# Two attention stages of a diffusion block: projections handed out in eighths behind the transposes, and scores that span two PSUM banks

## The chip, the cores and the metric

The kernel runs on one core of one Trainium2 chip. The metric is the time of one execution on the device, in microseconds (us). Three runs of the kernel before gave 2849.23, 2852.33 and 2855.4 us; their median, 2852.33 us, is the time to beat.

A core has five engines that work side by side, each through a queue of its own: TensorE (PE in the profile, with its weight loads as PEld), VectorE (DVE), ScalarE (ACT), GpSimd (POOL), and SyncE (SP), which issues transfers. TensorE writes to PSUM, which has eight banks of 512 float32 columns for each of 128 partitions. Semaphores order the engines among each other.

## The reference

Two layers run over 512 latent tokens and 256 context tokens of width 1024. Each layer has a feed-forward part, an attention part and another feed-forward part; the first layer's attention is grouped attention in a window, the second's is differential attention. Cut to what the change touches:

```python
def _gqa_window_mixer(...):            # 16 query heads, 4 key heads, 64 wide
    kx, vx = proj_kv(hx); kc, vc = proj_kv(hc)
    kx = _apply_rope(kx, cos, sin)
    qx = _apply_rope(proj_q(hx), cos, sin)
    # per block of 128 queries: 384 keys around it, and all of the context
    p = sink_softmax(concatenate([s_loc, s_ctx]))
    return einsum(p[..., :span], vb) + einsum(p[..., span:], vc)   # then @ w_out

def _diff_attn_mixer(...):             # 8 heads of two 64-wide halves, all 768 keys
    p = softmax(s * 64 ** -0.5)
    p = p[:, :, 0] - lam * p[:, :, 1]
    o = _rmsnorm(p @ v, subln_w) * (1.0 - lambda_init)             # then @ w_out
```

Everything is float32. The kernel gets this precision from TensorE by splitting an operand into a rounded high part and a low remainder, so that a product of two split operands takes three matmuls.

## The kernel before, in words

All activations lie transposed, 128 features on the partitions by 768 tokens (256 of the context, then 512), eight such blocks. xh and xl are the two parts of the normalized input. A projection (project_halves, line 265) makes 128 output features: weights() (line 48) loads 128 by 1024 weights on SP's queue (line 54), ScalarE rounds them (line 55) and GpSimd takes the remainder (line 56); then, for each half of the tokens, 8 blocks k times 3 products are summed in one PSUM bank. VectorE scales the bank by the norm (scaled_halves, line 288), and rope() (line 306) turns queries and keys.

**Grouped attention** (gqa, line 321) has eight PSUM banks in four pools: one bank for projections and outputs (pbig, tiles "half"), two for transposes, one for values, four for scores. The loop (line 556) runs 24 steps: 4 key groups by 6 blocks of 128 queries (4 latent, 2 context). In step i the scores of step i + 1 are traced first (scores, line 411), then a whole projection or a unit of the output projection if the tables of lines 539 to 541 name one for this step, then the values of step i (values, line 458). scores() makes up to two chunks for each of four heads, with maximum (line 434), exponential (line 441) and a normalization, three heads of four on GpSimd (line 454). values() takes the blocks of keys that the table XB (line 402) lists: four transposes (line 466), a rounded copy on ScalarE (line 469), the remainder on VectorE (line 470), two matmuls (lines 471 and 472). At step 18 xh and xl are given up, hT is loaded in their place (line 561), and the finished outputs of the first two groups come back from DRAM (line 501). out_proj (line 508) multiplies them by the output weights and adds into hT (line 302).

**Differential attention** (diff, line 586) has the same eight banks. For each of 8 heads the four query blocks' probabilities (probs, line 668) alternate with the next head's projections of keys, queries and values. A block has two score sets (j = 0, 1) of 768 keys, in two chunks of 384, a bank each. The maxima (line 680) are joined and scaled (line 683), each chunk is exponentiated (line 686), the sums are joined and inverted (lines 690 to 692), GpSimd scales the second set (line 694) and VectorE adds the two (line 695). values() (line 698) transposes and multiplies, and ends in a norm of the output, four operations of it on GpSimd (lines 721 to 724). For the last head parts of the output projection stand in place of projections. rope() has its sine product on GpSimd here (line 315).

**The order of the work.** The order on every engine's queue is fixed ahead of the run by a planner: it runs an estimate of the program and lets each engine take the first-traced instruction that is ready by that estimate, so work traced late can be issued early where its inputs and buffers allow. A tile is given out again when its readers are done. With issue_after(x) the instructions traced in a block are placed behind x on x's engine, without waiting for x to end.

## Time and profile before

| what | value |
|---|---|
| median of three runs | 2852.33 us (2849.23 to 2855.4) |
| the profiled execution's own time | 2853.44 us |
| span of the profile, first to last instruction | 2851.6 us |
| granted TensorE clock, mean | 0.991 |
| TensorE busy | 2759.4 us, 97% of the span |
| VectorE busy | 1525.4 us, 53% |
| GpSimd busy | 1279.3 us, 45% |
| ScalarE busy | 962.6 us, 34% |
| last stage of grouped attention's loop ends near | 920 us |
| differential attention stands at about | 2060 to 2470 us |

A row of the profile names the line of the kernel, the engine, the operation, and the tiles it writes and reads; times are microseconds unless a mean is given, which is in nanoseconds. A matmul's busy time overlaps the next one's, so a busy TensorE is not always one at its peak. A wait is put down to the semaphore that came last. The granted clock of TensorE is given as a share of full speed.

### The profile page before, as it was taken

Reading aid. Unit: us, or ns where it says so; the run is one execution under the profiler, and the core shown is the slowest. Engines: PE = TensorE matmul, PEld = TensorE weight load, DVE = VectorE, ACT = ScalarE, POOL = GpSimd, SP = SyncE. Lnnn points to the kernel's source line nnn. Section 1 sums busy time; section 2 is a strip of 40 time slices with the busy share of each in tenths; the row PEclk is TensorE's granted clock in tenths of the full one; section 3 lists DMA queues with packets and bytes.
Section 4 is the critical chain, followed back from the end, with each engine's and each line's share of the span. In section 5 each row is a group of like instructions: output and inputs, shape, how many; then the busy total and the mean of one; then the engine's idle time right before and its main releaser. Section 6 shows DMA issues by size and latency. Waiting matters only on the chain. (4 is left out here: it accounts for less than half of the span.)

```text
span 2851.6 us, 40866 instructions
## 1 busy us (share of the span) xinstructions
PE 2759.4 (97%) x16162; PEld 2578.0 (90%) x16162; DVE 1525.4 (53%) x2661; ACT 962.6 (34%) x1733; POOL 1279.3 (45%) x756
## 2 busy tenths in 40 slices
PE   6999999999899999999999999999999999899998
PEld 4999999989777999999999999999988887799998
DVE  8645455567887844444557333333567777422223
ACT  3212112245666422121233221221345655422223
POOL 1434333365433533333444434333555665555553
PEclk9999999999999999999999999999999999999999
DMA  7332432342331223223323233233232233233331
GB/s 277 107 127 97 140 111 98 123 138 81 84 127 38 89 85 117 86 85 121 94 81 111 84 104 102 71 115 115 73 99 82 82 90 121 73 100 93 101 103 45
DMA packets 105119, 290.09 MB, mean 102 GB/s; under 512 B 12512, under 2 KB 22880, under 8 KB 104928
## 3 DMA queue, kind: packets, MB, share of 16 engines
q1 hardware_dynamic: 104496, 287.37, 31.3%
q8 instruction: 128, 2.10, 0.3%
q14 instruction: 63, 0.52, 0.1%
q10 hardware_dynamic: 432, 0.11, 0.0%
HBM read 257.28 MB, written 12.06 MB: 94 GB/s over the span
## 5 line engine op out<-in xcount | busy, mean ns | idle before, releaser
L56 POOL TENSOR_TENSOR w_lo<-w_raw,w_hi 128x1024 fp32r<-128x1024 f32 (+2 forms) x377 | 804.1, 2133 | 1089.8 <-ACT w_hi L55 1066.9
L55 ACT CAST w_hi<-w_raw 128x1024 fp32r<-128x1024 f32 (+2 forms) x377 | 337.5, 895 | 1112.4 <-PE big L70 398.2
L257 PE MATMUL big<-xh,w_hi 128*128 128x384 f32 (+3 forms) x2816 | 689.8, 326 | 6.5 <-DVE xh L174 3.2
L257 PE MATMUL big<-xh,w_lo 128*128 128x384 f32 (+3 forms) x2816 | 688.7, 326 | 0.6 <-POOL w_lo L56 0.5
L257 PE MATMUL big<-xl,w_hi 128*128 128x384 f32 (+3 forms) x2816 | 686.8, 325 | 0.9 <-DVE xl L185 0.9
L257 PEld LDWEIGHTS big<-xh,w_hi 128*128 128x128 f32 x2816 | 499.4, 190 | 10.0 <-DVE tb L210 3.7
L131 DVE SCALAR_TENSOR_TENSOR ada_junk<-w_raw,s_bc 128x1024 f32<-128x1024 f32 x224 | 337.4, 1506 | 305.9 <-DMA w_raw<-ada_w 303.7
L257 PEld LDWEIGHTS big<-xl,w_hi 128*128 128x128 f32 x2816 | 496.8, 190 | 1.1 <-DVE xl L185 1.1
L257 PEld LDWEIGHTS big<-xh,w_lo 128*128 128x128 f32 x2816 | 494.6, 189 | 1.6 <-POOL w_lo L56 1.6
L262 DVE COPY bias<-big 128x2 f32<-128x2 f32 x176 | 27.6, 157 | 597.0 <-PE big L257 596.9
L68 PE MATMUL big<-hh,w_hi 128*128 128x512 f32 (+1 forms) x1200 | 327.4, 344 | 0.0
L72 PE MATMUL big<-hh,w_lo 128*128 128x512 f32 (+1 forms) x1200 | 326.8, 344 | 0.0
L70 PE MATMUL big<-hl,w_hi 128*128 128x512 f32 (+1 forms) x1200 | 326.8, 343 | 0.0
L302 DVE SCALAR_TENSOR_TENSOR hT<-big,mod,hT 128x512 f32<-128x512 f32 (+1 forms) x288 | 167.9, 618 | 180.9 <-PE big L72 180.6
L70 PEld LDWEIGHTS big<-hl,w_hi 128*128 128x128 f32 x1200 | 225.6, 188 | 30.0
L72 PEld LDWEIGHTS big<-hh,w_lo 128*128 128x128 f32 x1200 | 224.7, 188 | 28.8
L68 PEld LDWEIGHTS big<-hh,w_hi 128*128 128x128 f32 x1200 | 224.8, 188 | 27.1
L991 POOL TENSOR_TENSOR hl<-tb,hh 128x768 fp32r<-128x768 f32 (+1 forms) x88 | 151.5, 1722 | 169.9 <-ACT hh L990 158.1
L986 DVE SCALAR_TENSOR_TENSOR tb<-tb,bias,ta 128x512 f32<-128x512 f32 (+1 forms) x154 | 179.6, 1199 | 8.3 <-DVE tb L295 0.5
L276 PE MATMUL half<-xh,w_hi 128*128 128x384 f32 (+3 forms) x464 | 155.4, 335 | 20.3 <-DVE ta L288 18.2
L990 ACT CAST hh<-tb 128x768 fp32r<-128x768 f32 (+1 forms) x88 | 68.7, 781 | 268.4 <-DVE tb L986 268.4
L276 PE MATMUL half<-xl,w_hi 128*128 128x384 f32 (+3 forms) x464 | 153.7, 331 | 0.0
(224 smaller groups left out, 3595.6 us busy)
## 6 DMA issues: line engine op xcount, KB each, us to landing
w_raw<-ffn_gu SPq DMA_DIRECT2D x176, 512.0 KB, 3.3
w_raw<-ada_w SPq DMA_DIRECT2D x128, 512.0 KB, 3.3
w_raw<-ffn_d SPq DMA_DIRECT2D x96, 256.0 KB, 2.7
w_raw<-ffn_d SPq DMA_DIRECT2D x64, 320.0 KB, 2.9
w_raw<-diff_in SPq DMA_DIRECT2D x24, 512.0 KB, 3.2
w_raw<-gqa_in SPq DMA_DIRECT2D x12, 512.0 KB, 3.5
ada_raw<-ada_w SPq DMA_DIRECT2D x8, 512.0 KB, 9.4
ada_rawk<-ada_k SPq DMA_DIRECT2D x8, 512.0 KB, 7.8
```

The lines of the kernel that those rows point to most:

```text
L55: nc.scalar.copy(out=hi[:, :cols], in_=raw[:, :cols])
L56: nc.gpsimd.tensor_tensor(out=lo[:, :cols], in0=raw[:, :cols], in1=hi[:, :cols].bitcast(F32), op=ALU.subtract)
L68: nc.tensor.matmul(o, wh, xh, start=(k == 0), stop=False)
L70: nc.tensor.matmul(o, wh, xl, start=False, stop=False)
L72: nc.tensor.matmul(o, wl, xh, start=False, stop=(k == n - 1))
L131: getattr(nc, engines[s]).scalar_tensor_tensor(out=junk, in0=raw, scalar=1.0, in1=self.sbc[:, s], op0=ALU.mult, op1=ALU.mult, accum_out=se ...
L257: mm(ps[:, c, :e - s], w[:, k], x[:, k, s:e], start=first, stop=last)
L276: mm(ps[:, :e - s], w_[:, k], x[:, k, s:e], start=(k == 0 and i == 0), stop=(k == ND - 1 and i == 2))
L302: self.nc.vector.scalar_tensor_tensor(out=h, in0=o, scalar=self.mv(l, s, c, d), in1=h, op0=ALU.mult, op1=ALU.add)
L986: nc.vector.scalar_tensor_tensor(out=u[:, tk], in0=u[:, tk], scalar=bu[:, s:s + 1], in1=g[:, tk], op0=ALU.add, op1=ALU.mult)
L990: nc.scalar.copy(out=hh[:, toks], in_=u[:, toks])
L991: nc.gpsimd.tensor_tensor(out=hl[:, toks], in0=u[:, toks], in1=hh[:, toks].bitcast(F32), op=ALU.subtract)
```

## The change

In grouped attention a projection becomes a generator, scaled_steps: it yields after the three products of each k, so one projection is sixteen parts, eight for each half of the tokens, and the bank of a half is scaled as soon as it is full. out_proj gets the same form (paced): a unit is sixteen parts, the context's tokens first, then the latent ones, each with its own residual addition. values() calls the next parts itself: eight in a step, shared out over its key blocks, sixteen in step 23. They are traced after the block's four transposes and their copies, and placed behind the last of these transposes on TensorE. The eight projections follow one another from step 0; the four units of the output projection are set up at step 17, where the loads of hT and of the first two groups' outputs are traced too.

In differential attention the score pool has two tiles of two banks in place of four of one. One negated maximum over 768 keys and one exponential with one sum take the place of two each and of the joining operations; the factor 0.125 moves into the scaling of the queries. The scaling of the second set, the sine product of rope() and the norm after the values move from GpSimd to VectorE, the last as three operations. The first projections of this stage and its norm use the two-bank tiles (project_banks, norm_banks).

```diff
-    def project_halves(self, src, xonly=False, pool=None, tag="half"):
+    def project_banks(self, src, pool, xonly=False, scale=None):
+
+        ps = pool.tile([P, 2, 512], F32, name="s")
+        self.project_k([(self.weights(src), ps)], range(ND), xonly)
+        n = 256 if xonly else 384
+        return (ps[:, 0], ps[:, 1]), self.bias_of(ps[:, 1, n:n + 2], scale)
+
+    def bias_of(self, ps, scale=None):
+        bias = self.sp.tile([P, 2], F32, name="bias")
...
+    def norm_banks(self, pool):
+        ps = pool.tile([P, 2, 512], F32, name="s")
+        for i in range(2):
+            tk = slice(i * 384, i * 384 + 384)
+            self.nc.tensor.matmul(ps[:, i, :384], self.ones, self.acc[:, tk], start=True, stop=True)
+        for i in range(2):
+            tk = slice(i * 384, i * 384 + 384)
+            self.rsqrt(self.rstd[:, tk], ps[:, i, :384], 1.0 / D)
+
...
+    def scaled_steps(self, src, pool=None, tag="half"):
+
+        w = self.weights(src)
+        pool = pool or self.pbig
+        u = self.tp.tile([P, T], F32, name="ta")
+        for s, e in ((0, 384), (384, T + 2)):
+            ps = pool.tile([P, 512], F32, name=tag)
+            for k in range(ND):
+                for i, (w_, x) in enumerate(((w[0], self.xh), (w[0], self.xl), (w[1], self.xh))):
+                    self.nc.tensor.matmul(ps[:, :e - s], w_[:, k], x[:, k, s:e], start=(k == 0 and i == 0),
+                                          stop=(k == ND - 1 and i == 2))
+                if k < ND - 1:
+                    yield
+            bias = self.bias_of(ps[:, 384:386]) if s else None
+            self.nc.vector.tensor_tensor(out=u[:, s:s + 384], in0=ps[:, :384], in1=self.rstd[:, s:s + 384], op=ALU.mult)
+            if not s:
+                yield
+        return u, bias
...
+            if scale:
+                self.nc.vector.scalar_tensor_tensor(out=u[:, tk], in0=ps[i][:, :n], scalar=scale, in1=self.rstd[:, tk],
+                                                    op0=ALU.mult, op1=ALU.mult)
...
+            if early:
+                return self.scaled_halves(early[0], "ta"), early[1]
+            return (yield from self.scaled_steps(a["gqa_in"][i], pool, "s" if pool else "half"))
...
-            u, bias = project(i, pool)
+            u, bias = yield from project(i, pool)
...
-        def values(g, pp, qb):
+            return out, mm.ins
+
+        def values(g, pp, qb, left):
...
-                    nc.tensor.transpose(tr[:, o:o + P], pp[h][:, j * P:(j + 1) * P], self.ident)
+                    turned = nc.tensor.transpose(tr[:, o:o + P], pp[h][:, j * P:(j + 1) * P], self.ident)
...
+
+                with self.tc.issue_after(turned.ins):
+                    for _ in range(-(-left // (len(blocks) - j))):
+                        left -= 1
+                        other()
                 nc.tensor.matmul(av, vs[:, b, g], th, start=(j == 0), stop=False)
                 nc.tensor.matmul(av, vs[:, b, g], tl, start=False, stop=(j == len(blocks) - 1))
...
-                    for r in part:
-                        o = os_[r // 2]
-                        for w, c, first, last in ((wh, 0, r == 0, False), (wh, 1, False, False),
-                                                  (wl, 0, False, r == 3)):
-                            for ps, (s, tk) in zip(outs, cuts):
-                                mm(ps, w[:, i * 4 + r], o(c, r % 2)[:, tk], start=first, stop=last)
-                    if part[-1] == 3:
+
+                    for group in (((0,), (1,)) if paced else ((0, 1),)):
+                        for r in part:
+                            o = os_[r // 2]
+                            for w, c, first, last in ((wh, 0, r == 0, False), (wh, 1, False, False),
+                                                      (wl, 0, False, r == 3)):
+                                for n in group:
+                                    mm(outs[n], w[:, i * 4 + r], o(c, r % 2)[:, cuts[n][1]], start=first, stop=last)
+                            if paced and (r < 3 or group[0] == 0):
+                                yield
+                        if paced:
+                            self.residual(outs[group[0]:group[0] + 1], cuts[group[0]:group[0] + 1], 0, 5, d)
+                    if paced and i == 0:
+                        yield
+                    if part[-1] == 3 and not paced:
...
-        do_k(0, early)
-        do_q(0, pss)
-        do_q(1, pss)
-        do_v(0, pss)
-
-        fill = {0: ("q", 2), 2: ("q", 3), 4: ("k", 1), 6: ("q", 4), 8: ("q", 5), 10: ("v", 1), 12: ("q", 6),
-                15: ("q", 7)}
-        outs = {19: 0, 20: 1, 21: 2, 22: 3}
...
+        whole(do_k(0, early))
+        whole(do_q(0, pss))
+        whole(do_q(1, pss))
+        whole(do_v(0, pss))
+
+        todo = [do_q(2), do_q(3), do_k(1), do_q(4), do_q(5), do_v(1), do_q(6), do_q(7)]
...
-        def other(i):
-            if i in fill:
-                f, n = fill[i]
-                {"q": do_q, "k": do_k, "v": do_v}[f](n)
-            if i in outs:
-                out_proj(0, os_, (outs[i],))
-
-        pp = step(0)
+        def other():
+            try:
+                if todo:
+                    next(todo[0])
+            except StopIteration:
+                todo.pop(0)
...
-            if i == 18:
+            if i == 17:
                 self.xp.release()
                 self.h_open()
                 for d in range(ND):
                     nc.sync.dma_start(self.hT[:, d], self.hd[d])
                 o01 = self.sb("gqa_o", 1, side="right")
                 os_ = [load_o(o01, 0), load_o(o01, 1)]
+                todo = [out_proj(0, os_, (u,), paced=True) for u in range(4)]
+            if i == 18:
 
                 o3t = [rq.tile([P, T], F32R, name="qs") for _ in range(4)]
-            nxt = step(i + 1) if i < 23 else None
-            other(i)
-            values(g, pp, qb)
+            nxt = None
+            if i < 23:
+                nxt, mm = step(i + 1)
+            values(g, pp, qb, 8 if i < 23 else 16)
             pp = nxt
...
-        pss = self.ps("pdiff_s", 4)
+        pss = self.ps("pdiff_s", 2)
...
-        early = self.project_halves(a["diff_in"][8], pool=pss, tag="s")
-        self.norm_halves(pss)
+        early = self.project_banks(a["diff_in"][8], pss)
+        self.norm_banks(pss)
...
-            self.rope(u, bias, u[:, XT], nc.gpsimd)
+            self.rope(u, bias, u[:, XT])
...
+
+            ps, bias = (self.project_banks(a["diff_in"][h], pool, True, scale=0.125) if pool else
+                        self.project_halves(a["diff_in"][h], True, scale=0.125))
+            u = self.scaled_halves(ps, "ta", True, scale=0.125)
+            self.rope(u, bias, u[:, XT])
...
-            st = self.sp.tile([P, 12], F32, name="st4")
+
+            st = self.sp.tile([P, 6], F32, name="st4")
+            nm, sm, r = st[:, 0:2], st[:, 2:4], st[:, 4:6]
...
-                ss = []
-                for c in range(2):
-                    s = pss.tile([P, 512], F32, name="s")[:, :384]
-                    kc = ks[j][:, c * 384:(c + 1) * 384]
-                    nc.tensor.matmul(s, qs[j][0][:, qc], kc, start=True, stop=False)
-                    nc.tensor.matmul(s, qs[j][1][:, qc], kc, start=False, stop=True)
-                    nc.vector.tensor_reduce(out=st[:, 2 * j + c:2 * j + c + 1], in_=s, op=ALU.max, axis=AX.X)
-                    ss.append(s)
-                nm = st[:, 4 + j:5 + j]
-                nc.vector.tensor_scalar(out=nm, in0=st[:, 2 * j:2 * j + 1], scalar1=st[:, 2 * j + 1:2 * j + 2],
-                                        scalar2=-0.125, op0=ALU.max, op1=ALU.mult)
-                for c in range(2):
-                    nc.scalar.activation(out=p[:, c * 384:(c + 1) * 384], in_=ss[c], func=AF.Exp, bias=nm, scale=0.125,
-                                         accum_out=st[:, 6 + 2 * c + j:7 + 2 * c + j])
+                s = pss.tile([P, 2, 512], F32, name="s")[:, :, :384]
+                for i in range(2):
+                    for c in range(2):
+                        nc.tensor.matmul(s[:, c], qs[j][i][:, qc], ks[j][:, c * 384:(c + 1) * 384], start=(i == 0),
+                                         stop=(i == 1))
+                nc.vector.tensor_reduce(out=nm[:, j:j + 1], in_=s, op=ALU.max, axis=AX.XY, negate=True)
+                nc.scalar.activation(out=p.rearrange("p (c n) -> p c n", c=2), in_=s, func=AF.Exp, bias=nm[:, j:j + 1],
+                                     accum_out=sm[:, j:j + 1])
                 out.append(p)
-            r = self.sp.tile([P, 2], F32, name="rr")
-            nc.vector.tensor_tensor(out=r, in0=st[:, 6:8], in1=st[:, 8:10], op=ALU.add)
-            nc.vector.reciprocal(out=r, in_=r)
-            nc.vector.tensor_tensor(out=r[:, 1:2], in0=r[:, 1:2], in1=lam[:, 2:3], op=ALU.mult)
+            nc.vector.reciprocal(out=r, in_=sm)
             p0, p1 = out
-            nc.gpsimd.tensor_scalar(out=p1, in0=p1, scalar1=r[:, 1:2], scalar2=1.0, op0=ALU.mult, op1=ALU.mult)
+            nc.vector.tensor_scalar(out=p1, in0=p1, scalar1=r[:, 1:2], scalar2=lam[:, 2:3], op0=ALU.mult, op1=ALU.mult)
             nc.vector.scalar_tensor_tensor(out=p0, in0=p0, scalar=r[:, 0:1], in1=p1, op0=ALU.mult, op1=ALU.add)
...
-            nc.gpsimd.tensor_tensor(out=v, in0=v, in1=r0, op=ALU.mult)
-            nc.gpsimd.tensor_tensor(out=v, in0=v, in1=r0, op=ALU.mult)
-            nc.gpsimd.tensor_scalar(out=v, in0=v, scalar1=-0.5, scalar2=1.5, op0=ALU.mult, op1=ALU.add)
-            nc.gpsimd.tensor_tensor(out=r0, in0=v, in1=r0, op=ALU.mult)
+            nc.vector.tensor_tensor(out=v, in0=v, in1=r0, op=ALU.mult)
+            nc.vector.scalar_tensor_tensor(out=v, in0=v, scalar=-0.5, in1=r0, op0=ALU.mult, op1=ALU.mult)
+            nc.vector.scalar_tensor_tensor(out=r0, in0=v, scalar=1.5, in1=r0, op0=ALU.add, op1=ALU.mult)
```

42 lines of the change are left out of this document (23 added, 19 removed).

## The prediction, written before the run

> **What bounds the kernel now.** The page's first line gives the span; the view of busy time by stretch then shows in which stages TensorE is not full.
>
> ```profile
> span 2851.6 us, 40866 instructions
> 640.00:760.00 120.00, 115.93 (x700) 108.62 (x698) 92.90 (x229) 72.52 (x188) 62.62 (x52) 1.00 0.31 88
> 760.00:820.00 60.00, 50.01 (x272) 41.15 (x273) 51.33 (x139) 41.87 (x119) 26.33 (x29) 0.94 0.47 158
> 820.00:880.00 60.00, 59.48 (x368) 52.18 (x368) 51.15 (x135) 39.27 (x114) 23.64 (x27) 1.00 0.10 34
> 880.00:920.00 40.00, 33.94 (x189) 26.60 (x188) 29.15 (x77) 26.22 (x74) 14.86 (x24) 1.00 0.12 39
> 1000.00:1400.00 400.00, 400.00 (x2277) 384.09 (x2276) 181.26 (x262) 83.94 (x108) 154.61 (x76) 1.00 0.29 93
> 2100.00:2360.00 260.00, 243.19 (x1459) 227.24 (x1460) 195.77 (x427) 148.37 (x355) 154.60 (x105) 0.99 0.30 87
> 2360.00:2480.00 120.00, 105.61 (x532) 86.99 (x531) 72.58 (x117) 56.42 (x107) 64.96 (x40) 0.94 0.31 99
> ```
>
> The first pair of figures of a stretch is TensorE's busy time and its matmuls. The feed-forward stretch 1000 to 1400 has 400.00 of 400: nothing in the diff can shorten such a stage. The two attention stages have idle time. In the grouped loop (640 to 920) TensorE is busy 115.93 + 50.01 + 59.48 + 33.94 = 259.4 of 280, VectorE 224.5 (80%). The idle time sits in two stretches: 760 to 820 (50.01 of 60) and 880 to 920 (33.94 of 40); the other two hold 175.4 of 180, or 97.5%. In differential attention 2100 to 2360 has 243.19 of 260 and 2360 to 2480 has 105.61 of 120. So some 20.6 + 16.8 + 14.4 = 52 us can be had at most by the busy rows, somewhat more because a busy row also covers matmuls that are slowly fed.
>
> Next, the waits of TensorE in the grouped loop (us, times, longest), then in the differential loop.
>
> ```profile
> PE av L471 <- DVE o L479: 4.1, 4, 1.4
> PE av L471 <- ACT pth L469: 3.3, 4, 1.0
> ...
> PE half L276 <- DVE ta L288: 15.8, 13, 2.1
> PE s L678 <- ACT p L686: 0.4, 1, 0.4
> ```
>
> In the grouped loop no single wait rules: they are the softmax and value chain itself, met when nothing else is queued. In the differential loop one wait rules: the next half projection needs the single bank of the pool "half", which VectorE has not drained (15.8 us in 13 waits, while scores wait 0.4 us).
>
> Why has the grouped loop no filler at 760? The load queue and the first output projection answer it.
>
> ```profile
> 794.29 0.33 SPq L561 DMA_DIRECT2D hT<-hd  x1
> ...
> L526 PE MATMUL half<-og,w_hi x192: 278/387/484, 809.7 to 945.8; 128*128 128x256 f32 x96, 128*128 128x512 f32 x96
> ```
>
> hT takes the place of xh and xl, so its first load at 794.29 marks the last projection matmul. Reading lines 539 to 572, the planner put the projections, which were traced ahead of the values, as early as their buffers allowed; they were used up there, and the output projection could not start before its operands came back from DRAM (first matmul 809.7).
>
> **Grouped attention.** Removed: whole projections at eight places of the loop. Added: a generator that yields after each of eight k, so that a step gets half a projection, pinned behind the transposes of its value blocks. The work is the same: the same matmuls, drains, rope, casts and DMAs. One half is 24 matmuls. A timeline of the differential stage (start, us, engine) shows 24 in a row and what stands beside them.
>
> ```profile
> 2279.86 2.39 POOL L56 TENSOR_TENSOR w_lo<-w_raw,w_hi 128x1024 fp32r<-128x1024 f32 x1 [2.01 <-ACT w_hi L55]
> 2279.95 0.34 PE L276 MATMUL half<-xh,w_hi 128*128 128x384 f32 x1
> 2280.16 2.12 DVE L690 TENSOR_TENSOR rr<-st 128x2 f32<-128x2 f32 x1
> 2283.98 0.34 PE L276 MATMUL half<-xh,w_lo 128*128 128x384 f32 x1
> 2285.05 0.58 ACT L686 ACTIVATE p<-s,st 128x384 f32<-128x384 f32 x1
> 2285.76 0.54 DVE L690 TENSOR_TENSOR rr<-st 128x2 f32<-128x2 f32 x1 [1.54 <-ACT p L686]
> 2286.82 0.44 PE L276 MATMUL half<-xh,w_hi 128*128 128x386 f32 x1 [1.65 <-DVE ta L288]
> ```
>
> From the first of these matmuls to the last of 24 is 2283.98 - 2279.95 = 4.03 us, so 0.175 each and 4.2 us a half. Sixteen steps get 4.2 us each. The output projection of the first two groups is cut into 64 parts of three matmuls, eight a step over steps 17 to 22 and sixteen in step 23. The stretches at 760 and 880 therefore get filler. I price this by the loop's own good stretches: if all of it ran at 97.5%, 259.4 us of busy time would take 266, against 280, so 14 us less; the poor stretches were also slowly clocked (the column behind POOL's is the granted clock: 0.94 at 760), worth up to 0.06 x 60 = 3.6 us, of which I take 2. That is -16. VectorE would then be at 224.5 of 264, 85%; in 820 to 880 it was at 51.15 of 60, also 85%, with TensorE full, so the rate has been reached in this loop. Bounds: -20.6 (all idle time) less the clock's 3.6, so -24; on the other side what rival (a) prices.
>
> With a projection move its weight load on SP's queue, ScalarE's cast, GpSimd's subtraction and SP's swaps of half tiles (lines 365 to 367, 381 to 383). They come later than now, past the stores of lines 486 and 487, but the last query (step 15) still stands two steps, some 23 us, ahead of its group's first scores (traced in step 17): that covers them.
>
> A step is lost in between: the last part comes in step 15, the first of the output projection in step 17, and its operands queue behind eight hT loads. Before, 15.4 us passed from the first hT load to the first output matmul (794.29 to 809.7); a step takes 280 us / 24 = 11.7, so a wait of up to some 4 us is left, or none. I take +2. The single bank's drain between the halves now falls where scores and values can stand, so it costs nothing as long as they are ready; without that cover it is 16 waits of about 1 us.
>
> **Differential attention.** Per head of about 40 us (260 us for 6.5 heads) the removed and moved operations are these, VectorE, GpSimd and ScalarE:
>
> ```profile
> L680 DVE TENSOR_REDUCE st<-s 128x1 f32<-128x384 f32 x128 | 66.3, 548 | 10.6 <-PE s L679 10.4
> L683 DVE TENSOR_SCALAR st<-st 128x1 f32<-128x1 f32 x64 | 12.4, 202 | 0.1
> L690 DVE TENSOR_TENSOR rr<-st 128x2 f32<-128x2 f32 x32 | 17.1, 536 | 9.9 <-ACT p L686 9.9
> L692 DVE TENSOR_TENSOR rr<-rr,lam 128x1 f32<-128x1 f32 x32 | 13.0, 406 | 0.7
> L694 POOL TENSOR_SCALAR p<-p,rr 128x768 f32<-128x768 f32 x32 | 31.1, 971 | 58.4 <-DVE rr L692 52.3 <-ACT oh L727 1.8 <-DVE bias L280 1.6
> L315 POOL TENSOR_TENSOR tb<-tb,sin 128x512 f32<-128x512 f32 x14 | 18.6, 1327 | 2.7 <-DVE tb L313 1.9 <-DVE rr L692 0.8
> L721 POOL TENSOR_TENSOR hT<-hT 128x512 f32<-128x512 f32 x8 | 12.5, 1561 | 8.2 <-ACT hT L720 8.2
> L722 POOL TENSOR_TENSOR hT<-hT 128x512 f32<-128x512 f32 x8 | 10.9, 1363 | 0.5
> L723 POOL TENSOR_SCALAR hT<-hT 128x512 f32<-128x512 f32 x8 | 5.0, 623 | 0.2
> L724 POOL TENSOR_TENSOR hT<-hT 128x512 f32<-128x512 f32 x8 | 10.3, 1284 | 0.7
> L686 ACT ACTIVATE p<-s,st 128x384 f32<-128x384 f32 x128 | 73.2, 584 | 43.2 <-DVE st L683 43.2
> ```
>
> The rows nearest to what takes their place come from the grouped stage and the norm:
>
> ```profile
> L434 DVE TENSOR_REDUCE st<-s 128x1 f32<-128x256 f32 x64 | 26.0, 415 | 3.0 <-PE s L429 1.8 <-PE s L432 1.1
> L434 DVE TENSOR_REDUCE st<-s 128x1 f32<-128x512 f32 x32 | 21.6, 684 | 7.0 <-PE s L432 6.9
> L315 DVE TENSOR_TENSOR tb<-tb,sin 128x512 f32<-128x512 f32 x8 | 6.8, 856 | 0.2
> L441 ACT ACTIVATE p<-s,st 128x256 f32<-128x256 f32 x64 | 30.3, 477 | 2.5 <-PE tr L466 2.5
> L441 ACT ACTIVATE p<-s,st 128x512 f32<-128x512 f32 x32 | 21.9, 689 | 11.3 <-PE tr L466 7.2 <-DVE st L438 3.4 <-PE s L429 0.7
> L213 DVE SCALAR_TENSOR_TENSOR tb<-tb,ta 128x512 f32<-128x512 f32 x1 | 0.7, 691 | 0.0
> ```
>
> VectorE loses 16 x 0.548 + 8 x 0.202 + 4 x 0.536 + 4 x 0.406 = 14.2 us a head. It gains eight reductions over 768 elements; 512 against 256 cost 0.684 - 0.415 more, so 768 costs 0.95, 7.6 in all; two sine products at 0.86, 1.7; three norm operations at 0.69, 2.1; and four scalings of 768, not seen on VectorE: between the 0.2 of a tiny one (L683) and GpSimd's 0.97; I take 0.7, as for 512 in the norm, 2.8. Sum 14.2: level, from 12 to 15.3. The scale of 0.125 rides in drains that exist already. GpSimd loses 4 x 0.971 + 2 x 1.327 + 4.83 = 11.4 us a head of 23.8 (154.60 / 6.5), nearly half. ScalarE's exponentials go from 16 x 0.584 = 9.3 to 8 of 768 elements; by the same slope (0.212 for 256) each is 0.90, so 7.2.
>
> What reaches TensorE is the path in the timeline above: the last exponential starts at 2285.05, L690 waits for it 1.54 us and takes 0.54, then comes the drain, and the matmul at 2286.82 had waited 1.65 us. Two exponentials of 0.90 instead of four of 0.58 end 0.5 earlier, and L690 is gone, 0.5: about 1 us less a head, -7 over seven heads. Bounds: 0, and -15.8 if all those waits go. A two-bank score tile is freed only when its whole exponential is done, 0.3 us later than the first half was; with 0.4 us of waits of that kind now, and projections to run meanwhile, I add nothing; uncovered, 8 x 0.3 x 7 = +17.
>
> At the end of the stage nothing covers the last head's norm:
>
> ```profile
> PE o L746 <- ACT o L727: 3.9, 1, 3.9
> ...
> 2440.00:2460.00 20.00, 20.00 (x87) 16.26 (x87) 14.84 (x16) 10.61 (x15) 12.66 (x6) 0.85 0.24 79
> ```
>
> Four GpSimd operations (4.83 us) become three of VectorE (2.07): 2.8 us off a 3.9 us wait. The slice after it ran at a granted clock of 0.85, so 3 us were lost to clock; with a wait of 1 us I take half of that back, -1.5. The Trainium skill, "TensorE: Matmul & The Clock Gate" (What's actually happening), says the clock halves after about 3.4 us of idling and returns after as much work; by that rule the 3.9 us wait would cost a slow window and a 1 us wait none, so the whole 3 us would come back. The trace agrees so far that the slow slice stands right behind the wait. At the stage's start two-bank tiles let the next projection in only when both halves of the norm are read: one more reading of some 0.7, +1.
>
> The Trainium skill, "SBUF — State Buffer" (Who interferes with whom), says that VectorE and GpSimd share a port pair as an exclusive lock, and that a VectorE operation with two SBUF inputs waits for the whole GpSimd instruction that reads SBUF. The trace agrees: L690, two values wide, took 2.12 us while w_lo ran from 2279.86 for 2.39, against 0.54 when it ran later. By that rule the moved operations can be held too.
>
> **Sum.** Against the profiled execution's own 2853.44 us (span 2851.6; the runs' median is 2852.33, about 1 us below): -16 + 2 - 7 - 2.8 - 1.5 + 1 = -24.3, so 2829.
>
> **Rivals.** (a) The pins cost, and the kernel is slower. The planner fixes TensorE's order ahead of the run; before, a projection could stand ahead of a transpose whose probabilities are late, and now its parts stand behind it. There are 88 groups of transposes (22 blocks for each of four groups by the table in lines 402 to 409). If each exposes w us and the filling brings nothing, the time is 2853.4 - 10.3 + 88 w: slower than before from w = 0.12; at 0.3, 2869. For it: av waits 3.3 and 4.1 us even now. Against: probabilities are made one step ahead, and scores of the next step may pass. 10%.
> (b) VectorE is the true bound of the grouped loop: at 80% busy, held by the order of its queue, it can't be fed faster when projections and heavy steps coincide; only 2 us are gained there beside the differential 10: 2841. For it: 51.33 of 60 busy at 760, where TensorE starves. Against: 820 to 880. 20%.
> (c) Both stages fill: the grouped one -24, the differential one -15.8 - 2.8 - 3 - 4 for loop waits that aren't single: 2804. For it: TensorE at 59.48 of 60 in one stretch. Against: no cure for the single bank in the differential loop. 13%.
> (d) The nine moved VectorE operations a head are held while GpSimd works: it stays busy (23.8 - 11.4) / 40 = 31% of the time; half of w_lo's 2.39 each gives 9 x 0.31 x 1.2 = 3.3 us a head, +23 over seven, against what the removed L690 and L692 took beyond the 0.20 of L683, a scalar operation like them: 4 x (0.34 + 0.20) x 7 = 15. That is +8 in place of -7: 2844. For it: L690 held for 2.12 us. Against: GpSimd itself is freer. 9%.
>
> **Chances.** The forecast holds 48%. About 0.2% is what a measurement can tell, 2846.7 to 2858. Faster: 48, 13, nearly all of (b), most of (d): 80%. Same: what is left of these and the mild side of (a), 9%. Slower: 11%. The range runs from (c)'s side, with some room, 2796, to 2856, where (a) begins.
>
> **What would show it.** Right: busy share near 97% in all of the grouped loop, half matmuls spread to its end, its VectorE near 85%; no stretch like 760 to 820; in the differential loop the waits of half on ta below 10 us, GpSimd near 12 us a head, reductions of about 0.95; the wait on oh near 1 us. Wrong: waits of transposes or av on VectorE or ScalarE growing past 10 us in the grouped loop (a); VectorE over 90% with TensorE idle (b); moved operations with means well above 0.7 to 0.9 (d).

## The result, and the profile after

The changed kernel takes 2869.89 us (median of four runs, 2866.69 to 2873.49) against 2853.86 us of the kernel before beside it (2849.23 to 2856.69): a ratio of 1.0058, with a 95% interval of 1.0039 to 1.0077. It is **slower by 16 us** (0.6%). The forecast was 2829 with a range up to 2856. The profiled execution took 2869.55 us.

The view of busy time by stretch, of the kernel after, in the same columns as before: time, length, then busy time (and count) of TensorE, its weight loads, VectorE, ScalarE and GpSimd, the granted clock, the share of the DMA engines and GB/s.

```profile
640.00:760.00 120.00, 107.17 (x609) 97.97 (x608) 92.44 (x239) 71.68 (x197) 51.41 (x49) 0.91 0.25 69
760.00:820.00 60.00, 52.28 (x295) 47.98 (x294) 45.96 (x113) 36.26 (x98) 27.27 (x27) 0.91 0.24 69
820.00:880.00 60.00, 48.33 (x241) 39.99 (x239) 42.02 (x97) 32.17 (x84) 23.23 (x24) 0.83 0.41 143
880.00:920.00 40.00, 36.88 (x225) 31.38 (x226) 32.95 (x91) 25.52 (x81) 13.90 (x17) 1.00 0.04 14
920.00:980.00 60.00, 57.28 (x325) 48.39 (x324) 40.59 (x66) 32.17 (x62) 28.14 (x24) 1.00 0.19 62
2360.00:2480.00 120.00, 112.22 (x598) 95.79 (x597) 84.03 (x122) 61.46 (x103) 42.17 (x20) 1.00 0.33 105
...
640.00:660.00 20.00, 15.43 (x73) 13.89 (x72) 10.42 (x26) 8.79 (x22) 9.38 (x5) 0.79 0.45 122
720.00:740.00 20.00, 14.31 (x65) 13.02 (x66) 15.50 (x40) 9.91 (x30) 11.06 (x10) 0.74 0.44 118
860.00:880.00 20.00, 15.53 (x49) 11.63 (x47) 7.38 (x15) 4.63 (x10) 3.77 (x4) 0.57 0.63 230
```

The same view of the kernel before, for a slice that the prediction did not show:

```profile
720.00:740.00 20.00, 19.15 (x117) 18.11 (x116) 17.84 (x43) 13.89 (x37) 10.15 (x10) 1.00 0.31 90
```

To compare stretches I count as lost the idle time of TensorE plus its busy time times (1 - granted clock). From 640 to 980 the kernel before loses 4.1 + 13.0 + 0.5 + 6.1 + 0 = 24 us (its TensorE is busy for all of 920 to 980) and the kernel after 22.5 + 12.4 + 19.9 + 3.1 + 2.7 = 61 us. (The clock is rounded to a hundredth, so a stretch is good to about half a us. The difference of 37 us is more than the 30 that this loop turns out to cost: a busy row is not always fed at the full rate, so the count shows where time went, and only roughly how much.) The poor stretch at 760 did not fill, and three slices that had been full or nearly so are now the worst: 640 to 660 lost 7.8 us, 720 to 740 lost 9.4, 860 to 880 lost 11.2 (all of 820 to 880 had lost 0.5 before). From 2360 to 2480, in differential attention, TensorE is busier than before, 112.22 against 105.61, though the changed kernel reaches this stage later, so the two stretches don't hold quite the same work.

What stands at 720? A timeline of the kernel after (start, us, engine, line, operation) follows the fourth query, q3, from the last matmul of its projection to the first score that needs it:

```profile
704.15 0.34 PE L314 MATMUL half<-xh,w_lo 128*128 128x386 f32 x1
...
705.76 0.45 PE L474 MATMUL s<-kh,qs 128*128 128x512 f32 x1
...
718.35 0.51 SPq L413 DMA_DIRECT2D qs<-ta  x1
...
721.30 0.50 PE L474 MATMUL s<-kh,qs 128*128 128x512 f32 x1 [1.37 <-DMA qs<-ta]
```

Step 6 is the first of key group 1. Its first two heads use q2, its last two q3. The scores of the second head start at 705.76, and those of the third at 721.30: 15.5 us later, when the swap of line 413 has landed. In the kernel before the same chain took about as long (12.8 us from the projection's last matmul at 672.27 to the issue of the last swap, against 14.2 here), but stood far ahead of its use; here is its last swap, and the first score of the same step:

```profile
685.09 0.46 SPq L367 DMA_DIRECT2D qs<-ta  x1
...
719.70 0.47 PE L428 MATMUL s<-kh,qs 128*128 128x512 f32 x1
```

So the query's lead, from its last swap to the scores of its step, went from 35 us to nothing, and the chain of rotation, cast, subtraction and swaps, some 17 us from matmul to matmul (721.30 - 704.15), now lies on the path once per key group. From 640 to 920 the scores' waits for a free bank (for the exponential that empties it) grew from 2.5 us in 4 waits to 9.3 in 11, and waits for a query's transfer are new:

```profile
PE s L474 <- ACT p L487: 9.3, 11, 3.5
...
PE s L474 <- DMA qs<-ta: 4.7, 3, 2.7
```

Why the lead went is seen best at the last change of key group. Step 15's parts, the last of q7, hang on the transposes of step 15; a timeline of TensorE there:

```profile
844.84 0.28 PE L474 MATMUL s<-kh,qs 128*128 128x256 f32 x1
...
849.23 0.60 PE L512 MATMUL tr<-ident,p 128*128 128x128 f32 x4
...
850.55 0.34 PE L314 MATMUL half<-xh,w_lo 128*128 128x386 f32 x1
...
851.54 0.47 PE L474 MATMUL s<-kh,qs 128*128 128x512 f32 x1
...
877.06 0.40 PE L474 MATMUL s<-kh,qs 128*128 128x512 f32 x1
```

Line 474 at 844.84 is the end of step 17's scores; it stands ahead of step 15's last transposes (849.23, line 512). On TensorE's queue the transposes of a step lag its scores by two steps. A part that hangs on the transposes of step 15 is therefore next to the scores of step 18, not two steps ahead of them: 850.55 and 851.54 are neighbours. The third head of step 18 had to wait until 877.06.

In differential attention the groups after stand as follows (line, engine, operation, tiles, shape, count, busy us and mean ns, idle before):

```profile
L748 DVE TENSOR_REDUCE st<-s 128x1 f32<-128x768 f32 x64 | 59.2, 950 | 10.7 <-PE s L746 10.4
...
L749 ACT ACTIVATE p<-s,st 128x768 f32<-128x768 f32 x64 | 57.6, 903 | 10.6 <-DVE st L748 7.6 <-PE tr L763 2.4
...
L755 DVE SCALAR_TENSOR_TENSOR p<-p,st,p 128x768 f32<-128x768 f32 x32 | 38.5, 1202 | 0.8
...
L754 DVE TENSOR_SCALAR p<-p,st,lam 128x768 f32<-128x768 f32 x32 | 23.0, 718 | 0.8
...
L749 ACT ACTIVATION_READ_ACCUMULATOR p<-s,st 128x1 f32 x64 | 12.6, 196 | 0.0
```

and TensorE's waits there (us, times, longest):

```profile
PE half L300 <- DVE ta L330: 6.9, 6, 1.2
PE half L300 <- DVE ta L333: 6.7, 7, 2.7
PE o L805 <- ACT o L786: 1.3, 1, 1.3
```

The prices of these operations came out as worked: 0.950 us for a reduction (0.95), 0.903 for an exponential (0.90), 0.718 for the scaling (0.7). One did not: the last of the three norm operations (line 783) takes 1.150 us, where 0.69 was taken for each; the other two take 0.69. The wait for the last norm is 1.3 us, where 3.9 had been and 1 was expected. The wait of the half projections for their bank is 13.6 us in 13 waits over the whole stage (2060 to 2480), against 17.4 in 14 before: less, but not below 10.

### The profile page after: what moved, and what is told of

Read it like the earlier page. It is cut to its first block, busy times and chain, and to the rows that moved or that the text cites. A ratio compares the mean times of both kernels' runs of the same rounds, so it can differ in the third digit from the quotient of the medians.

```text
span 2867.7 us, 40548 instructions
## 1 busy us (share of the span) xinstructions
PE 2763.6 (96%) x16162; PEld 2585.3 (90%) x16162; DVE 1539.4 (54%) x2541; ACT 952.2 (33%) x1605; POOL 1189.6 (41%) x676
## 4 chain that ended last, share of the span: by engine, by line
PE 87%; DVE 6%; DMA 3%; ACT 2%; issue 1%; POOL 1%; SPq 0%; DVEq 0%; POOLq 0%; ACTq 0%
PE big L257 47%; PE big L68 7%; PE big L72 7%; PE big L70 7%; PE half L300 5%; PE half L579 2%; PE half L314 2%; PE s L746 1%; PE tr L512 1%; PE s L257 1%; DMA ql<-ql 1%; DVE ada_junk L897 1%; PE tr L763 1%; DVE st L480 1%; PE s L474 1%
## 5 line engine op out<-in xcount | busy, mean ns | idle before, releaser
L257 PEld LDWEIGHTS big<-xh,w_hi 128*128 128x128 f32 x2816 | 499.2, 190 | 11.2 <-DVE tb L210 4.8
L1043 ACT ACTIVATE ta<-ta,bias 128x512 f32<-128x512 f32 (+1 forms) x154 | 90.1, 626 | 122.0 <-DVE ta L340 122.0
L300 PE MATMUL half<-xh,w_hi 128*128 128x384 f32 (+3 forms) x336 | 110.1, 328 | 13.7 <-DVE ta L330 6.9
```

The source lines that it names most:

```text
L257: mm(ps[:, c, :e - s], w[:, k], x[:, k, s:e], start=first, stop=last)
L300: mm(ps[:, :e - s], w_[:, k], x[:, k, s:e], start=(k == 0 and i == 0), stop=(k == ND - 1 and i == 2))
L1043: nc.scalar.activation(out=g[:, tk], in_=g[:, tk], func=AF.Silu, bias=bg[:, s:s + 1])
```

## The experiments

All are timed beside the kernel before on the same chip, and each computes the whole reference. The kernel before took 2852.2 to 2853.9 us (medians) in all of these rounds, so times of different rounds can be compared to about 1 us, beside their own scatter. Diffs are against the changed kernel unless another is named, and cut to what matters.

### Which half of the change costs

The grouped loop as changed and differential attention as before:

```diff
     def diff(self, after):
...
-        pss = self.ps("pdiff_s", 2)
+        pss = self.ps("pdiff_s", 4)
...
```

> The grouped stage as changed, the differential stage as before. The changed kernel's trace reaches its differential stage about 31 us later than before and spends about 17 us less in it. If the two parts simply add, this run takes some 31 us more than before: 2885 us (2878 to 2891). If the loss came from something common to both (clock, load queue), it would lie nearer the changed kernel's 2870.

Measured: 2883.39 us (2879.84 to 2885.89), ratio 1.0102 [1.0087, 1.0117], so +29.8 us against 2853.57.

And the other way round, the grouped loop as before, differential attention as changed:

```diff
...
-        todo = [do_q(2), do_q(3), do_k(1), do_q(4), do_q(5), do_v(1), do_q(6), do_q(7)]
+        fill = {0: ("q", 2), 2: ("q", 3), 4: ("k", 1), 6: ("q", 4), 8: ("q", 5), 10: ("v", 1), 12: ("q", 6),
+                15: ("q", 7)}
...
```

> The differential stage as changed, the grouped stage as before. If the parts add: 17 us less than before, 2837 us (2831 to 2843). The prediction had put this part at 10 us. If the gain of the differential stage only hides time lost ahead of it, about 2854.

Measured: 2839.99 us (2838.55 to 2842.39), ratio 0.9953 [0.9937, 0.9970]: -13.6 us. The two add to +16.2, and the change did +16.0. So the halves add, the loss is all in the grouped loop, and this second kernel is the fastest of all that were run, ahead of both the kernel before and the changed one.

### The pins, or the lead of the queries

Without the pins, the parts are free in the order of the queue:

```diff
-                with self.tc.issue_after(turned.ins):
+                with nullcontext():
```

> The changed kernel, but the parts of projections are not placed behind the transposes; they are still traced in eighths with the values. Theory A (the pins make queries too late and leave no filler where a key group changes): the planner can issue them ahead again, the three stalls at the changes of key group and the one at the loop's start (about 8, 9, 14 and 18 us of TensorE time) mostly vanish, 2870 less about 40: 2830 (2822 to 2845). Theory B (the eighths themselves, with one bank and a drain per half, cost the time, pinned or not): about 2870.

Measured: 2846.01 us (2843.91 to 2848.43), ratio 0.9975 [0.9964, 0.9986]. The pins cost 24 us of the 30: theory A's direction, but only 24 of the 40 us that it expected, just outside its range. It is some 6 us slower than the kernel with the old grouped loop (2839.99; the intervals overlap a little), so even unpinned the cutting gained nothing.

With the pins, but the third query's projection whole ahead of the loop, which puts each later part two steps earlier:

```diff
         whole(do_v(0, pss))
...
+        whole(do_q(2))
...
-        todo = [do_q(2), do_q(3), do_k(1), do_q(4), do_q(5), do_v(1), do_q(6), do_q(7)]
+        todo = [do_q(3), do_k(1), do_q(4), do_q(5), do_v(1), do_q(6), do_q(7)]
```

> The changed kernel, pins kept, but the first of the eight projections of the loop is done whole ahead of the loop, so that every later one ends two steps earlier; nothing is left for steps 14 to 16. Theory A1 (what is missing is the lead of the queries at the three changes of key group, about 40 us together): most of the three stalls goes, some of it returns in the steps without filler: 2845 (2835 to 2855). Theory A2 (pins block the filler wherever probabilities are late, the lead does not matter): 2865 to 2880.

Measured: 2850.84 us (2847.62 to 2855.99), ratio 0.9992 [0.9982, 1.0001]. All pins of the remaining parts are in place and 19 us are back, as theory A1 expected. One stretch, two of the three worst slices and, in a timeline, one query's path in this kernel:

```profile
640.00:760.00 120.00, 106.46 (x630) 97.96 (x629) 94.98 (x233) 71.40 (x190) 56.99 (x51) 0.97 0.29 79
...
720.00:740.00 20.00, 19.05 (x122) 18.03 (x121) 18.95 (x42) 15.03 (x39) 12.27 (x11) 1.00 0.52 144
...
860.00:880.00 20.00, 20.00 (x130) 17.80 (x128) 18.44 (x48) 14.72 (x43) 8.71 (x10) 1.00 0.00 1
```

```profile
691.34 0.34 PE L314 MATMUL half<-xh,w_lo 128*128 128x386 f32 x1
...
715.31 0.45 PE L474 MATMUL s<-kh,qs 128*128 128x512 f32 x1
```

q3's last matmul is at 691.34, and the first score that needs it runs at 715.31 with no wait for a transfer: 24 us from matmul to score, which covers the 17 us of the chain. The slices that had stood at the loop's start and at two changes of key group are full again (640 to 660 too, with 20.00 of 20), all at the full clock. The lost time of 640 to 760 falls from 22.5 to 13.5 + 0.03 x 106 = 16.7. So the larger part of the loss is the missing lead, shown by giving it back with the pins kept; 11 us are left against the old grouped loop.

### What the other 11 us are

The projections whole and free as before, and only the output projection in pinned parts:

```diff
-        todo = [do_q(2), do_q(3), do_k(1), do_q(4), do_q(5), do_v(1), do_q(6), do_q(7)]
+        todo = []
+        fill = {0: (do_q, 2), 2: (do_q, 3), 4: (do_k, 1), 6: (do_q, 4), 8: (do_q, 5), 10: (do_v, 1), 12: (do_q, 6),
+                15: (do_q, 7)}
...
-            values(g, pp, qb, 8 if i < 23 else 16)
+            if i in fill:
+                f, n = fill[i]
+                whole(f(n))
+            values(g, pp, qb, (8 if i < 23 else 16) if i > 16 else 0)
```

> The changed kernel, but the eight projections are traced whole and unpinned, at the places of the loop that they had before; only the output projection of the first two groups stays cut into 64 parts, pinned behind the transposes of steps 17 to 23. Theory A (the loss is the lead of queries, keys and values alone, and late parts of the output projection are useful filler, since nothing in the loop waits for them): the end of the grouped loop fills, some 3 to 6 us below the kernel with only the differential change (2840.0), so 2834 to 2838. Theory B (pinning behind the transposes costs wherever it is done, since it takes away the freedom to put a matmul ahead of a late transpose): 2844 to 2850.

Measured: 2853.14 us (2851.31 to 2857.84), ratio 1.0002 [0.9993, 1.0010]: 13 us slower than with the old placement (2839.99), theory B and more. The stretch at 820 and the group of the output matmuls (durations in ns, then first and last start) of this kernel:

```profile
820.00:880.00 60.00, 51.55 (x292) 42.23 (x290) 47.75 (x131) 38.74 (x115) 18.95 (x25) 0.91 0.02 7
```

```profile
L579 PE MATMUL half<-og,w_hi x192: 276/386/500, 857.4 to 958.4; 128*128 128x256 f32 x96, 128*128 128x512 f32 x96
```

and the same two of the kernel with the old grouped loop:

```profile
820.00:880.00 60.00, 59.45 (x370) 52.17 (x369) 50.97 (x136) 39.27 (x113) 23.89 (x27) 1.00 0.10 33
```

```profile
L571 PE MATMUL half<-og,w_hi x192: 277/376/484, 811.3 to 947.9; 128*128 128x256 f32 x96, 128*128 128x512 f32 x96
```

Free, its first matmul runs at 811.3, and it fills 820 to 880 (59.45 of 60). The operands are not what is late: the loads of hT begin at 794.90 there and at 796.47 with the old loop, and those of the first groups' outputs lie as near. Pinned behind step 17, it waits until 857.4 while TensorE stands idle or slowly clocked for 13 us of that stretch, and the last parts end 10 us later. A pinned part can't be used before its own step, whatever hole opens there.

Two more placements tried the opposite cure. The whole schedule two steps earlier, output parts over steps 16 to 23:

```diff
+        whole(do_q(2))
...
-            if i == 17:
+            if i == 15:
                 self.xp.release()
...
-                todo = [out_proj(0, os_, (u,), paced=True) for u in range(4)]
+                early_out = [out_proj(0, os_, (u,), paced=True) for u in range(4)]
+            if i == 16:
+                todo = early_out
...
-            values(g, pp, qb, 8 if i < 23 else 16)
+            values(g, pp, qb, 8)
```

> The changed kernel with the parts pinned as they are, but two steps earlier throughout: the third query's projection whole before the loop (2850.8 so far), and now also the release of xh and xl and the loads of hT and of the output projection's operands two steps earlier (step 15), and the 64 output parts over steps 16 to 23, eight in each. Theory A (beside the lead, what is left is the bunching of the parts: steps 14 to 16 without any, sixteen in the last): 3 to 6 us less than 2850.8, 2845 to 2848. Theory B (what is left is that a pinned part can't fill a hole in another step): within 2 us of 2850.8.

Measured: 2853.35 us (2847.94 to 2857.55), ratio 1.0001 [0.9992, 1.0010], no gain on 2850.84. That is theory B's side, half a us outside its 2.

Projections in pinned parts with their lead, as in the run that gave back 19 us, and the output projection whole and free at its old steps:

```diff
+        whole(do_q(2))
...
-            if i == 17:
+            if i == 18:
                 self.xp.release()
...
-            values(g, pp, qb, 8 if i < 23 else 16)
+            if i in outs:
+                whole(out_proj(0, os_, (outs[i],)))
+            values(g, pp, qb, 8 if i < 16 else 0)
```

> The changed kernel with the third query's projection whole before the loop (2850.8, with every later part two steps earlier), and the output projection of the first two groups whole and unpinned, traced at the steps that it had before (19 to 22). Theory A (two separate costs: the lead of the queries, which is cured here, and pinned output parts that can't fill the holes before their own steps, 13 us by the run with only these pinned): 2838 to 2842. Theory B (the holes at steps 11 to 17 are there whichever way the output projection is placed, and the 13 us came from taking its operands a step earlier): 2846 to 2852.

Measured: 2848.21 us (2845.31 to 2852.56), ratio 0.9987 [0.9978, 0.9996]. The number is in theory B's range, but B's reason for the 13 us, operands taken a step earlier, does not fit the run with the free projections, where they were not late. It is 2.6 us below the kernel with pinned output parts, and the intervals overlap, so freeing the output projection gave little, not 11. The costs of pinned projections (8 us here) and of pinned outputs (13 us above) don't add to the 11 of both. The traces show why the output projection could not help here: hT takes the place of xh and xl, so its loads wait for the last matmul of a projection. With the projections free that matmul runs at 796.28 (old grouped loop, first output matmul at 811.3); pinned, with their lead, it runs at 827.71 in this kernel (first output matmul at 842.3). A pinned projection holds xh and xl some 30 us longer, and the free output projection starts as much later.

Last, pinned filler where the kernel before starved: only q6 and q7 in pinned parts, over steps 10 to 13, the rest free:

```diff
+        todo = []
+        fill = {0: (do_q, 2), 2: (do_q, 3), 4: (do_k, 1), 6: (do_q, 4), 8: (do_q, 5), 9: (do_v, 1)}
+        outs = {16: 0, 18: 1, 20: 2, 22: 3}
...
-            if i == 17:
+            if i == 10:
+                todo = [do_q(6), do_q(7)]
+            if i == 14:
                 self.xp.release()
...
+            values(g, pp, qb, 8 if 10 <= i < 14 else 0)
```

> The differential change, and in the grouped loop everything whole and unpinned as before except the last two queries' projections, which are cut into 16 parts each and pinned behind the transposes of steps 10 to 13, where TensorE starved in the kernel before (760 to 820); hT and the operands are loaded from step 14 and the output projection is traced from step 16. Both queries still end more than three steps ahead of their group's scores. Theory A (paced filler helps where the lead is kept): 2 to 6 us less than 2840.0, 2834 to 2838, the best so far. Theory B (the holes move on to where the output projection now starts later): 2840 to 2846.

Measured: 2846.63 us (2843.04 to 2852.32), ratio 0.9979 [0.9970, 0.9988]; theory B's side, a little beyond its range, and 7 us slower than 2839.99. Its stretches:

```profile
640.00:760.00 120.00, 112.12 (x658) 102.65 (x658) 95.02 (x241) 73.19 (x193) 62.58 (x54) 0.99 0.31 88
760.00:820.00 60.00, 53.15 (x302) 45.22 (x302) 48.84 (x123) 38.98 (x112) 19.65 (x24) 0.97 0.14 42
820.00:880.00 60.00, 53.67 (x303) 45.40 (x303) 50.85 (x131) 39.62 (x114) 25.25 (x29) 0.91 0.37 133
```

The stretch at 760 did improve, from 50.01 to 53.15 at a better clock (4.6 us less lost than in the kernel before). But 640 to 760 gave up 4.9 and 820 to 880 10.6: the parts came out of the first, and the output projection, which needs the place of xh and xl, started later in the second (last projection matmul at 822.85, first output matmul at 838.4). The filler is a fixed amount; moved into one hole it is missing in another.

### SP's queue

At the third change of key group the swaps of q7 stand behind twelve loads on SP's queue in the changed kernel (start, us of issuing):

```profile
850.74 4.31 SPq L622 DMA_DIRECT2D hT<-hd  x8
855.15 3.44 SPq L552 DMA_DIRECT2D og<-god  x4
...
864.08 0.48 SPq L411 DMA_DIRECT2D qs<-qs  x1
...
872.36 0.46 SPq L413 DMA_DIRECT2D qs<-ta  x1
```

The third swap, which writes what the first reads, is issued 8.3 us after it; at 715.80 to 718.35, with no such loads, it took 2.6. With the eight loads on ScalarE's queue:

```diff
-                    nc.sync.dma_start(self.hT[:, d], self.hd[d])
+                    nc.scalar.dma_start(self.hT[:, d], self.hd[d])
```

> The changed kernel, with the eight loads of hT at step 17 issued from ScalarE's queue in place of SP's. In the changed kernel they take 4.3 us of issuing on SP ahead of the swaps of the last query, for which the scores of group 3 wait. Theory A (queue order is a part of the loss): 3 to 5 us less at the third change of key group, 2865 to 2867. Theory B (the swaps are late only because the query's projection is): within 1.5 us of the changed kernel's 2869.9.

Measured: 2866.22 us (2862.99 to 2868.34), ratio 1.0044 [1.0032, 1.0056], 3.7 us less than the change: theory A's number, though the intervals overlap. Its trace, of an execution of 2868.34 us, the slowest of its five, agrees in part: the third head's score of that step comes at 873.94, where it came at 877.06. But the third swap is issued only 1.1 us earlier (871.29), since the first now comes later (866.30): ScalarE, which casts the query ahead of the swaps, issues the last three loads for 5.84 us from 856.05 and executes nothing else meanwhile.

The same edit in the kernel with the old grouped loop:

> The grouped loop as before and the differential change, with the eight loads of hT issued from ScalarE's queue. With a lead of 47 us for the last query, SP's queue holds nothing that is waited for, so theory A (queue order costs only where the lead is gone) expects 2840 within 1.5 us. Rival (the loads on SP also delay the output projection's operands): 2 to 4 us less, 2836 to 2838.

Measured: 2845.66 us (2841.99 to 2849.15), ratio 0.9977 [0.9968, 0.9986], not better but 5.7 us worse than 2839.99, with intervals that just touch. Neither text foresaw that. Where the query has its lead, the move helps nothing. Why it costs is not shown: in this kernel the issues on ScalarE are short, 0.33 to 0.81 us.

### The two parts of the differential change

Two-bank scores alone, with the grouped loop as before; the scaling, the sine product and the norm stay on GpSimd (the norm's lines are left out here):

```diff
-            self.rope(u, bias, u[:, XT])
+            self.rope(u, bias, u[:, XT], nc.gpsimd)
...
-            nc.vector.tensor_scalar(out=p1, in0=p1, scalar1=r[:, 1:2], scalar2=lam[:, 2:3], op0=ALU.mult, op1=ALU.mult)
+            nc.vector.tensor_tensor(out=r[:, 1:2], in0=r[:, 1:2], in1=lam[:, 2:3], op=ALU.mult)
+            nc.gpsimd.tensor_scalar(out=p1, in0=p1, scalar1=r[:, 1:2], scalar2=1.0, op0=ALU.mult, op1=ALU.mult)
```

> The kernel before with one part of the differential change: scores over two banks with one reduction and one exponential each, the scale in the drains of the queries, L690's sum gone; the rotation's sine product, the scaling of p1 and the norm stay on GpSimd, and lambda's multiplication stays on VectorE. By the prediction's terms (-7 from a shorter softmax chain, +1 at the start): -6, 2847.5. Rival (the softmax chain is worth nothing, since the single bank is drained late for another reason, GpSimd's part of it): -1 to +1, 2853 to 2855.

Measured: 2844.53 us (2843.28 to 2849.24), ratio 0.9969 [0.9957, 0.9981]: -9.1 us, where -6 was expected.

The moves from GpSimd to VectorE alone, scores in one bank each; the diff is against the kernel before:

```diff
-            self.rope(u, bias, u[:, XT], nc.gpsimd)
+            self.rope(u, bias, u[:, XT])
...
-            nc.gpsimd.tensor_scalar(out=p1, in0=p1, scalar1=r[:, 1:2], scalar2=1.0, op0=ALU.mult, op1=ALU.mult)
+            nc.vector.tensor_scalar(out=p1, in0=p1, scalar1=r[:, 1:2], scalar2=lam[:, 2:3], op0=ALU.mult, op1=ALU.mult)
```

> The kernel before with the other part of the differential change: the scores and their softmax as before in one bank each, but the rotation's sine product, the scaling of p1 (with lambda in it, so L692 is gone) and the norm run on VectorE in place of GpSimd. By the prediction's terms (last norm -2.8, clock behind it -1.5, no cost of the moved operations): -4.3, 2849.3. The two parts would then add to -10.3 where -13.6 was measured, so 3 us more are in one of them or in both together. Rival (d) (moved operations are held by GpSimd and load VectorE): +2 to +8, 2856 to 2862, and all of the gain is in the two-bank scores.

Measured: 2856.66 us (2854.60 to 2863.80), ratio 1.0014 [1.0006, 1.0022]: +3.0 us, at the near end of rival (d)'s range. Alone, the parts make -6.1; together they made -13.6. The stretch 2060 to 2480 of the kernel before, of two-bank scores alone, of the moves alone, and of both:

```profile
2060.00:2480.00 420.00, 384.92 (x2201) 346.98 (x2200) 295.29 (x580) 222.81 (x488) 246.06 (x158) 0.98 0.30 91
```

```profile
2060.00:2480.00 420.00, 391.02 (x2271) 357.81 (x2270) 270.79 (x426) 215.52 (x368) 250.40 (x162) 0.98 0.32 94
```

```profile
2060.00:2480.00 420.00, 381.85 (x2177) 344.56 (x2176) 328.51 (x617) 224.00 (x488) 158.51 (x79) 0.98 0.30 91
```

```profile
2060.00:2480.00 420.00, 393.88 (x2333) 360.63 (x2332) 300.64 (x465) 215.94 (x366) 167.80 (x83) 0.99 0.32 95
```

The third busy time is VectorE's: 295 before, 271 with two-bank scores, 329 with the moves, 301 with both. The moves load the engine on which the drains of the projections stand, and the two-bank scores make room for them there. That this is why the two together are worth more than their sum is not shown. TensorE's waits for the drained half bank don't bear it out: 17.4 us before, 11.6 with two-bank scores, 18.9 with the moves and 13.6 with both, so the moves add some 2 us to them either way. (The trace of two-bank scores alone is of an execution of 2849.24 us, the slowest of its six.) No run changed VectorE's load alone, and the cause of the extra 7.5 us stays open.

## Why the prediction was wrong, point by point

**The grouped loop, -16 + 2, measured +29.8.** The step that failed is this sentence: "the last query (step 15) still stands two steps, some 23 us, ahead of its group's first scores (traced in step 17): that covers them." It counted the lead in the order of tracing, at a mean step of 11.7 us. On TensorE's queue the scores of a step stand two steps ahead of its transposes, and the parts hang on the transposes. The lead is about 1 us (850.55 to 851.54), and the same holds for q3 (704.15 to the group's first score at 705.15) and q5 (779.5 to 780.3). The changed kernel shows the chain exposed; giving back two steps of lead returned 19 us of the 30.

The price itself, the whole loop at 97.5%, failed too. It took the good stretches as something that parts spread evenly would extend to the poor ones. But the kernel before already had all of its filler in the loop; six runs that placed it otherwise, with a lead for the queries, took 2846 to 2853 us, against 2840 with the old placement, and moved the holes. A good stretch was good because the free order had put more filler there. Pacing the projections to step 15 also moved the last reading of xh and xl from 794 to 851 us, and with it the first output matmul from 810 to 866; the prediction priced +2 for this place.

**Behind the loads of hT.** "a wait of up to some 4 us is left": the step from the first load (850.74) to the first output matmul (865.59, in the changed kernel) took 14.9 us, as the 15.4 measured before. What was missed is whom else these loads delay, the swaps behind them on SP's queue (3.7 us between the medians of the run that moved eight of them away and of the change, not clear of their intervals). The prediction named the queue and let the two steps of lead cover it.

**Rival (a), the pins,** had the right sign. Its 2869 at w = 0.3 is close to 2869.89 by accident: it spread the price over 88 groups of transposes, while the rows show most of it at the loop's start and at the changes of key group (28 us lost in three slices of 20 us), and its sign, waits of transposes or av past 10 us, did not appear (9.1 and 7.8 us on VectorE and ScalarE from 640 to 920). Rivals (b) and (c) expected gains in the loop; none was found. The sign of (b), VectorE over 90% busy with TensorE idle, did not appear either: it is busy 213.4 us of 280 after, 224 before.

**Differential attention, -10.3, measured -13.6.** The prices of the operations were right to about 0.02 us, but for the norm's last (1.150 for 0.69). Of the terms, the last norm (-2.8) is borne out by the wait of 3.9 us that became 1.3, with the moves alone too, while two-bank scores alone leave it at 3.9. The clock behind it (-1.5) was too small: the slice behind the wait stood at 0.85 before; in the kernel with the old grouped loop and the differential change every slice from 2380 to 2480 has the full clock, this one among them:

```profile
2440.00:2460.00 20.00, 17.58 (x127) 16.04 (x126) 9.90 (x12) 10.29 (x15) 15.90 (x8) 1.00 0.26 79
```

So all of the 3 us came back, of which the prediction had taken half. The -7 of the shorter softmax chain was mis-sized and mis-split: with the +1 of the start, -6 was forecast for two-bank scores, and they alone did -9.1; the moves, priced at -4.3, alone cost 3.0; together they gain 7.5 more than the sum of the two. The wait from which the -7 was read fell by 5.8 us with two-bank scores alone (17.4 to 11.6), so the other 3 us came from elsewhere. Rival (d) fits the moves alone in size: the norm's and the clock's terms should have given some 4 to 6 us (2.6 for the wait, 1.5 to 3 for the clock), so by this estimate the moved operations cost 7 to 9 us there. One gain was not in the sum at all: the operation that joins the two sets,

```profile
L695 DVE SCALAR_TENSOR_TENSOR p<-p,rr,p 128x768 f32<-128x768 f32 x32 | 51.6, 1619 | 7.2 <-POOL p L694 7.2
...
L686 ACT ACTIVATION_READ_ACCUMULATOR p<-s,st 128x1 f32 x128 | 26.2, 205 | 0.0
```

took 1619 ns before and takes 1202 (line 755, above), 13 us of VectorE over 32 calls, without being changed. The Trainium skill, "SBUF — State Buffer" (Who interferes with whom), says that a VectorE operation with two SBUF inputs contends with a GpSimd operation that reads SBUF. The traces agree, instance by instance. In a timeline of the kernel before,

```profile
2151.61 2.36 POOL L56 TENSOR_TENSOR w_lo<-w_raw,w_hi 128x1024 fp32r<-128x1024 f32 x1
2151.69 3.10 DVE L695 SCALAR_TENSOR_TENSOR p<-p,rr,p 128x768 f32<-128x768 f32 x1
```

it starts 0.08 us behind a GpSimd subtraction and takes 3.10 us. Taking the calls that a timeline lists singly (26 of 32 before, all after): where it overlaps no GpSimd instruction it takes 1.00 to 1.02 us, in the kernel before as in the changed one; where it overlaps one for at least half of its time it takes 1.95 us on average before and 1.81 after. After the change 18 of its 32 calls overlap none. How long GpSimd is busy does not tell its mean by itself: with the moves alone GpSimd is busy 158.51 us of the stretch, less than with both (167.80), and the mean is 1451 ns. I used that rule only against the change.

## What to carry to other kernels

Count the lead of an operand on the queue of the engine that uses it, from the rows of the trace, not in steps of the source: where scores run two steps ahead of values, work hung on the values is two steps late for the scores. Filler is a fixed amount; pinning it to a step forbids its use in every earlier hole, so pin only what nothing waits for, what has no hole ahead of it, and what holds no place that later work needs. And where a change has two independent halves, time each by itself: here one was worth 13.6 us and the other cost 29.8.

## What the runs showed of the hardware

**A stall is paid twice.** In the slice from 860 to 880 of the changed kernel, 4.5 of the 11.2 lost us are idle and 6.7 are the clock at 0.57. A timeline of TensorE there:

```profile
856.96 0.87 PE L512 MATMUL tr<-ident,p 128*128 128x128 f32 x3 [3.13 <-DVE ptl L516]
...
871.79 1.22 PE L579 MATMUL half<-og,w_hi 128*128 128x512 f32 x2 [0.58 <-DVE hT L347]
...
876.65 0.57 PE L579 MATMUL half<-og,w_lo 128*128 128x512 f32 x1
877.06 0.40 PE L474 MATMUL s<-kh,qs 128*128 128x512 f32 x1
```

After the wait of 3.13 us, matmuls of 512 columns take 0.57 us and more until 876.65, and 0.40 again from 877.06: about 17 us at the low rate, though no later wait is longer than 1.6 us. The Trainium skill, "TensorE: Matmul & The Clock Gate" (What's actually happening), gives about 3.4 us of idling to lose the clock and about 3.4 us of sustained work to regain it. Here a wait of 3.13 us, a little under the first figure, had the low rate behind it. The return took from 871.79, where the last short wait ended, to 877, some 5 us; that the short waits kept the clock low before that fits this trace, but no run tested it. The prediction counted the clock only as something to win back, 2 us.

**Each sum that ScalarE accumulates is read out by an instruction of its own**, 205 ns (line 686, above, 128 of them before). Half as many exponentials saved 26.2 - 12.6 = 13.6 us of ScalarE beside the 15.6 (73.2 - 57.6) of the exponentials themselves; the prediction had counted only the latter.
